# dt in the state-space units: multiplied per head into the product of decay and C·B

## The chip, the core and the metric

The kernel runs on one core of one Trainium2 chip. The time is the device time of one execution in microseconds; the median of several executions counts. Engines are named as in the profile: PE is TensorE, DVE is VectorE, ACT is ScalarE, POOL is GpSimd, SP is the engine that issues most of the DMAs; PEld is PE's loading of weights.

## What is computed

One layer of a decoder: a combined projection of 512 tokens, three token mixers side by side (DSA, NSA and a Mamba-2 state-space mixer, SSD), a gated sum and a feed-forward block. The change lies in the SSD mixer: 4 groups g of 8 heads, 4 chunks c of 128 tokens.

```python
def ssd_mixer(z, xbc, dt, conv_w, conv_b, dt_bias, a_log, d_skip, norm_g):
    ...
    seg = a_cum[:, :, :, None] - a_cum[:, :, None, :]
    lmat = jnp.exp(jnp.where(tril, seg, -jnp.inf))
    cb = jnp.einsum('bcign,bcjgn->bcijg', cm, bm)
    y_diag = jnp.einsum('bcijg,bcijgh,bcjgh,bcjghp->bcighp', cb, lmat, dtc, xs)
    decay_states = jnp.exp(a_cum[:, :, -1:] - a_cum)
    states = jnp.einsum('bcjgn,bcjgh,bcjghp->bcghpn', bm, decay_states * dtc, xs)
    ...
    y_off = jnp.einsum('bcign,bcghpn,bcigh->bcighp', cm, h_in, jnp.exp(a_cum))
    y = y_diag + y_off + xs * d_skip.reshape(SSD_GROUPS, SSD_HPG)[:, :, None]
    ...
    y = rms_norm(y * jax.nn.silu(z.astype(jnp.float32)), norm_g)
```

In y_diag, cb, the decay lmat, dt and x are multiplied and summed over the tokens j of the chunk. dt hangs on j and the head, as x does.

## The kernel before

The program is one stream of Python generators. `main()` runs the mixers one after the other: DSA, then SSD (`ssd`), then NSA. `filler()` makes the projections, the causal convolution, and later the branch and output projections. After each step of `main()` a loop lets `filler()` take steps until its share of work, a number that the step yields, is paid back. What is so recorded is then put in order for each engine by a scheduler with a timing of its own (`schedule_with_timeline_sim=True`), so a changed instruction can move others on every queue. PE runs its queue in the order given.

In the trace the SSD stage covers about 385 to 570 us. It has 16 units, one for a group and a chunk, numbered 0 to 15 here, in the order (0,0), (1,0), (0,1), (1,1) up to (1,3), then the same with groups 2 and 3. The fillers beside it are projections: groups of three products L451, L452 and L453 of 128x512 on PE, whose weights DVE splits at L172.

A unit works on chunk-by-chunk tiles with tokens on the partitions. `stage1` loads B, C (bcx) and the cumulated decays, spread to 128 partitions for 8 heads (E, three buffers). `load_xz` (L1257, issued by SP) loads x and z of the unit into one tile xz, of which there are two buffers: `u.xs` is its x half and `u.zs` its z half. `stage2` makes C·B in PSUM (`cbm`, tile name pv, L1264), masks E on POOL (L1265), takes eight exps on ACT (L1268, one per head) and multiplies E by `cbm` on DVE (L1275). POOL makes xt, x times dt (L1270, tile of its own, two buffers), xw for the state (L1273, not for the last chunk) and xd, x times the skip gain, which overwrites x (L1277).

`stage3` has the products of the state (L1286 reads it, L1293 makes the next one) and, for each of 8 heads, a 128x64 product of E and xt into the PSUM tile `py` (tile name sc, L1303). In the trace each head's product has two records. Then DVE adds the other terms (L1307) and multiplies by z (L1308), ACT squares the result for the norm and writes the square over z (L1309), and later PE transposes yv (L1314) for the store. The load of the unit after the next takes this unit's xz buffer, so it is issued after L1309.

The x of groups 2 and 3 are made by fillers while the units run: convolution on ACT and DVE (L821 to L828, its result is craw), transposes on PE (L835), a copy on ACT (L837) and a store that `load_xz` reads.

Of the kernel before, what the change touches and what calls it, by code (L numbers as in the profile page):

```python
# [7 lines left out]
F32 = mybir.dt.float32  # L8
F32R = mybir.dt.float32r
AF = mybir.ActivationFunctionType  # L10
ALU = mybir.AluOpType
# [29 lines left out]
def build_kernel(ctx, tc, A, out):  # L41
    nc = tc.nc
    pe, act, dve, pool = nc.tensor, nc.scalar, nc.vector, nc.gpsimd
# [5 lines left out]
    def bc(ap, shape):  # L49
        return ap.to_broadcast(shape)  # L50
# [6 lines left out]
    def popen(name, side="left", space=None, bufs=1):  # L57
        kw = dict(name=name, bufs=bufs, side=side)
        if space is not None:
            kw["space"] = space  # L60
            kw.pop("side")
        cm = tc.tile_pool(**kw)
        p = cm.__enter__()
        open_pools[name] = cm
        return p
# [24 lines left out]
    def ps(tag, shape, dt=F32, bufs=2):  # L90
        if tag == XT[0]:
            XT[1] += 1
            if XT[1] % 3 == 0:
                tag = "pF"
        return psp.tile(shape, dt, tag=tag, name=tag, bufs=PSB[tag])
# [17 lines left out]
    xt = []  # L113
# [1123 lines left out]
    def ssd(sv, ratio):  # L1237
        sp = popen("ssd", side="right")
        ssq = cp.tile([128, 4, 4], F32, name="ssq_y")
        col = lambda a, c, g: a[:, c * 32 + g * 8:c * 32 + g * 8 + 8]  # L1240
# [19 lines left out]
        def stage2(u):  # L1260
            g, c = u.g, u.c
            x3 = lambda a: a.rearrange("p (h d) -> p h d", d=64)
            cbm = ps("pv", [128, 512])[:, :128]
            pe.matmul(cbm, u.b[:, 0], u.b[:, 1], start=True, stop=True)  # L1264
            pool.affine_select(out=u.E, in_=u.E, compare_op=ALU.is_ge, fill=NEG, base=0,  # L1265
                               pattern=[[0, 8], [1, 128]], channel_multiplier=-1)
            for h in range(8):
                act.activation(u.E[:, h], u.E[:, h], AF.Exp, bias=col(sv["nac"], c, g)[:, h:h + 1])  # L1268
            u.xt = sp.tile([128, 512], F32, name="xt", bufs=2)
            pool.tensor_tensor(x3(u.xt), x3(u.xs), bc(col(sv["dth"], c, g)[:, :, None], [128, 8, 64]), op=ALU.mult)  # L1270
            if c < 3:
                u.xw = sp.tile([128, 512], F32, name="xw", bufs=2)
                pool.tensor_tensor(x3(u.xw), x3(u.xs), bc(col(sv["dw"], c, g)[:, :, None], [128, 8, 64]), op=ALU.mult)  # L1273
            yield ratio * 300
            dve.tensor_tensor(u.E, u.E, bc(cbm[:, None, :], [128, 8, 128]), op=ALU.mult)  # L1275
            u.xd = u.xs
            pool.tensor_tensor(x3(u.xd), x3(u.xs), bc(dskip[:, g * 8:g * 8 + 8][:, :, None], [128, 8, 64]), op=ALU.mult)  # L1277
            yield ratio * 300

        def stage3(u):  # L1280
            g, c = u.g, u.c
            x3 = lambda a: a.rearrange("p (h d) -> p h d", d=64)
            py = ps("sc", [128, 512])
            if c:
                po = ps("sc", [128, 512])
                pe.matmul(po, u.b[:, 1], hst[g], start=True, stop=True)  # L1286
                t1 = sp.tile([128, 512], F32, name="t1", bufs=2)
                dve.tensor_tensor(x3(t1), x3(po), bc(col(sv["ea"], c, g)[:, :, None], [128, 8, 64]), op=ALU.mult)
                pool.tensor_tensor(t1, t1, u.xd, op=ALU.add)
                yield ratio * 858  # L1290
            if c < 3:
                pst = ps("pT", [128, 512])
                pe.matmul(pst, u.b[:, 2], u.xw, start=True, stop=True)  # L1293
                hn = sp.tile([128, 512], F32, name="hst", bufs=4)
                if c == 0:
                    act.activation(hn, pst, AF.Copy)
                else:
                    pool.tensor_tensor(x3(hn), x3(hst[g]), bc(col(sv["dec"], c, g)[:, :, None], [128, 8, 64]), op=ALU.mult)
                    dve.tensor_tensor(hn, hn, pst, op=ALU.add)
                hst[g] = hn  # L1300
                yield ratio * 858
            for h in range(8):
                pe.matmul(py[:, h * 64:h * 64 + 64], u.E[:, h], u.xt[:, h * 64:h * 64 + 64], start=True, stop=True)  # L1303
                if h % 4 == 3:
                    yield ratio * 856
            yv = sp.tile([128, 512], F32, name="yv", bufs=2)
            dve.tensor_tensor(yv, py, t1 if c else u.xd, op=ALU.add)  # L1307
            dve.tensor_tensor(yv, yv, u.zs, op=ALU.mult)  # L1308
            act.activation(u.zs, yv, AF.Square, accum_out=ssq[:, c, g:g + 1])  # L1309

            def tr():
                pt = ps("pT", [128, 4, 128])
                for k in range(4):
                    pe.transpose(pt[:, k], yv[:, k * 128:k * 128 + 128], ident)  # L1314
                ev = sp.tile([128, 4, 128], F32, name="yev", bufs=2)
                for k in range(4):
                    act.activation(ev[:, k], pt[:, k], AF.Copy, scale=gcol[:, 4 * g + k:4 * g + k + 1])
                nc.sync.dma_start(yc_d[g, c], ev.rearrange("p k q -> p (k q)"))
            TR.append(tr)
            yield ratio * 100  # L1320
# [14 lines left out]
        yield from need(1)  # L1335
        load_xz(us[1])
        yield from stage2(us[0])
        for i in range(16):
            yield from need(i + 2)
            if i + 1 < 16:  # L1340
                yield from stage2(us[i + 1])
            if TR:
                TR.pop()()
                yield ratio * 436
            yield from stage3(us[i])
            if i + 2 < 16:
                load_xz(us[i + 2])
# [405 lines left out]
```

## Time and profile before

| | us |
|---|---|
| median of 3 runs | 1395.9 |
| lowest, highest | 1394.72, 1400.18 |
| profiled execution | 1403.27 |
| its span | 1401.5 |
| PE busy in the span | 1369.0 (98%) |
| DVE, ACT, POOL busy | 1001.1, 722.0, 286.8 |
| mean granted clock of PE, share of full | 0.986 |

The span is the profiled execution from its first to its last instruction. PE's clock has two levels, 1.2 and 2.4 GHz; the profile gives the granted clock of a stretch as a share of the higher one. An engine's busy time says little on its own here: what an edit is worth is read from the waits of PE in the stretch that it touches.

### The profile page before, as it was taken

To read this page: it belongs to the slowest core of one execution; us is meant where nothing else is said; L and a number is where in the kernel's file an instruction comes from. 1 tells how busy PE (TensorE), PEld (TensorE's weight loads), DVE (VectorE), ACT (ScalarE), POOL (GpSimd) and SP (SyncE) were. 2 spreads that over 40 slices of the span, in tenths; PEclk is the share of its full clock that TensorE was granted. 3 is DMA by queue.
4 is the path that set the end of the run, shared out by engine and by line. 5 is a ranking of instruction groups with operands and counts; after the bars stand their busy time and mean duration, and the time that the engine had idled before them with its cause. 6 is when DMAs were issued, how large, how long until landed. Compare 5 with 4: busy or idle time off the path is not lost.

```text
span 1401.5 us, 19674 instructions
## 1 busy us (share of the span) xinstructions
PE 1369.0 (98%) x6875; PEld 1142.1 (81%) x6875; DVE 1001.1 (71%) x1962; ACT 722.0 (52%) x1434; POOL 286.8 (20%) x235
## 2 busy tenths in 40 slices
PE   8989999999999999999999999999899999999998
PEld 7878888888877778888887888788789888888887
DVE  6499977999877656477667788888635575767841
ACT  5545436667666756366565566555224444444430
POOL 3445211111047375100000002133100201102000
PEclk9999999999999999999999999999999999999999
DMA  6335654644486687735435453435444665746531
GB/s 192 89 96 144 166 179 132 166 113 123 121 259 223 190 257 201 188 100 140 114 114 157 118 146 111 122 117 177 143 150 140 118 177 127 174 116 132 157 117 52
DMA packets 222721, 205.35 MB, mean 147 GB/s; under 512 B 15497, under 2 KB 170013, under 8 KB 222622
## 3 DMA queue, kind: packets, MB, share of 16 engines
q1 hardware_dynamic: 206652, 180.49, 43.7%
q0 software_dynamic: 15232, 20.98, 8.2%
q10 hardware_dynamic: 738, 2.63, 0.6%
q8 instruction: 54, 0.88, 0.3%
q14 instruction: 45, 0.37, 0.1%
HBM read 167.56 MB, written 36.51 MB: 146 GB/s over the span
## 4 chain that ended last, share of the span: by engine, by line
PE 77%; DVE 7%; DMA 7%; issue 4%; POOL 3%; ACT 2%; SPq 0%; DVEq 0%; POOLq 0%; ACTq 0%
PE pj L451 18%; PE pj L453 18%; PE pj L452 18%; PE sc L451 3%; PE sc L452 3%; PE sc L453 3%; DMA gld<-g_d 3%; PE pT L931 2%; PE sc L893 2%; PE sc L892 2%; PE pv L944 2%; DMA wraw<-in_w_in_dram 1%; PE pv L943 1%; POOL mixf L1488 1%; PE sc L1303 1%
## 5 line engine op out<-in xcount | busy, mean ns | idle before, releaser
L170 ACT ACTIVATE whi<-wraw 128x1024 fp32r<-128x1024 f32 (+2 forms) x190 | 198.3, 1048 | 233.8 <-PE pj L452 115.7
L172 DVE TENSOR_TENSOR wlo<-wraw,whi 128x1024 fp32r<-128x1024 f32 (+1 forms) x169 | 215.7, 1280 | 104.5 <-ACT whi L170 102.9
L451 PE MATMUL pj<-hTh,whi 128*128 128x512 f32 x384 | 153.6, 400 | 0.2 <-DVE cacc L824 0.2
L453 PE MATMUL pj<-hTh,wlo 128*128 128x512 f32 x384 | 152.6, 397 | 0.0
L452 PE MATMUL pj<-hTl,whi 128*128 128x512 f32 x384 | 152.3, 397 | 0.0
L451 PE MATMUL pj<-whi,hTh 128*128 128x512 f32 (+2 forms) x352 | 138.7, 394 | 5.9 <-DVE stk L521 3.2
L901 ACT ACTIVATE p<-p,nb,rs 128x256 f32<-128x256 f32 (+3 forms) x192 | 123.2, 645 | 30.6 <-DVE nb L899 30.6
L453 PE MATMUL pj<-whi,hTl 128*128 128x512 f32 (+2 forms) x352 | 137.8, 392 | 0.1
L452 PE MATMUL pj<-wlo,hTh 128*128 128x512 f32 (+2 forms) x352 | 137.6, 391 | 0.0
L451 PE MATMUL pj<-yh,whi 128*128 128x512 f32 (+1 forms) x288 | 109.7, 387 | 11.0 <-DVE gld L1485 6.4
L452 PE MATMUL pj<-yl,whi 128*128 128x512 f32 (+1 forms) x288 | 109.2, 379 | 0.0
L453 PE MATMUL pj<-yh,wlo 128*128 128x512 f32 (+1 forms) x288 | 108.9, 378 | 0.0
L452 PE MATMUL pj<-h2l,whi 128*128 128x512 f32 (+1 forms) x256 | 96.3, 376 | 0.0
L453 PE MATMUL pj<-h2h,wlo 128*128 128x512 f32 (+1 forms) x256 | 96.2, 376 | 0.0
L451 PE MATMUL pj<-h2h,whi 128*128 128x512 f32 (+1 forms) x256 | 96.1, 376 | 0.0
L987 POOL DMA_DIRECT2D qu<-q_d x32 | 23.5, 735 | 334.9 <-PE sc L893 259.3
L451 PEld LDWEIGHTS pj<-hTh,whi 128*128 128x128 f32 x384 | 72.4, 189 | 14.0 <-DVE cacc L824 0.4
L452 PEld LDWEIGHTS pj<-hTl,whi 128*128 128x128 f32 x384 | 72.4, 189 | 13.8 <-issue 0.5
L453 PEld LDWEIGHTS pj<-hTh,wlo 128*128 128x128 f32 x384 | 72.4, 189 | 13.8 <-issue 0.2
L451 PEld LDWEIGHTS pj<-whi,hTh 128*128 128x128 f32 x352 | 67.4, 192 | 19.8 <-issue 5.8
L935 ACT ACTIVATE pth<-pT 128x512 fp32r<-128x512 f32 x95 | 54.5, 592 | 47.4 <-PE pT L931 46.9
L453 PEld LDWEIGHTS pj<-whi,hTl 128*128 128x128 f32 x352 | 67.4, 191 | 12.4 <-DVE hTl L427 0.4
(385 smaller groups left out, 3294.9 us busy)
## 6 DMA issues: line engine op xcount, KB each, us to landing
wraw<-in_w_in_dram SPq DMA_DIRECT2D x84, 512.0 KB, 4.7
wraw<-in_w_ff_dram SPq DMA_DIRECT2D x58, 512.0 KB, 4.3
qd<-in_w_ff_dram POOLq DMA_DIRECT2D x18, 512.0 KB, 6.0
q_d<-qev SPq DMA_DIRECT2D x64, 128.0 KB, 2.5
qu<-q_d POOLq DMA_DIRECT2D x32, 256.0 KB, 3.7
E<-ac_d SPq DMA_DIRECT2D x16, 512.0 KB, 4.9
xz<-xz_d SPq DMA_DIRECT2D x16, 512.0 KB, 5.8
gld<-g_d SPq DMA_DIRECT2D x32, 256.0 KB, 2.8
```

Of the source, the lines that this page charges most:

```text
L170: act.activation(hi[:, :m], r[:, :m], AF.Copy)
L172: (pool if i in LOWP else dve).tensor_tensor(lo[:, :m], r[:, :m], f(hi[:, :m]), op=ALU.subtract)
L451: pe.matmul(o, lh, rh, start=first, stop=False)
L452: pe.matmul(o, lh, rl, start=False, stop=False)
L453: pe.matmul(o, ll, rh, start=False, stop=last)
L892: pe.matmul(s_[:, h % w, :n], u.q[h], kh[:, :n], start=True, stop=False)
L893: pe.matmul(s_[:, h % w, :n], u.q[h], kl[:, :n], start=False, stop=True)
L901: act.activation(u.p[h][:, :n], u.p[h][:, :n], AF.Exp, bias=u.nb[:, h:h + 1], scale=rs8[:, u.b, u.h0 + h:u.h0 + h + 1], accum_out=u.sm[:, ...
L931: pe.transpose(pt[:, h], u.p[h][:, kb * 128:kb * 128 + 128], ident)
L935: act.activation(ph, ptf, AF.Copy)
L944: pe.matmul(o, vk, pl0, start=False, stop=en)
L987: pool.dma_start(q.rearrange("p (i a) c -> p i (a c)", i=2), src)
```

## The change

POOL's product of x and dt (xt) is dropped. DVE's one product of E and C·B per unit, 128x1024, becomes eight instructions of 128x128, one for each head, that multiply E by the head's column of dt (dt's index j lies on the partitions of E) and by `cbm`. PE's products read x itself from xz. xd, which overwrote x, gets a tile of its own with two buffers, in the place that xt had. Lines after the removed one shift: L1273 is L1271, L1275 is L1274, L1277 is L1276, and L1286 to L1314 are one less.

```diff
--- before.py
+++ after.py
@@ -1266,14 +1266,13 @@
                                pattern=[[0, 8], [1, 128]], channel_multiplier=-1)
             for h in range(8):
                 act.activation(u.E[:, h], u.E[:, h], AF.Exp, bias=col(sv["nac"], c, g)[:, h:h + 1])
-            u.xt = sp.tile([128, 512], F32, name="xt", bufs=2)
-            pool.tensor_tensor(x3(u.xt), x3(u.xs), bc(col(sv["dth"], c, g)[:, :, None], [128, 8, 64]), op=ALU.mult)
             if c < 3:
                 u.xw = sp.tile([128, 512], F32, name="xw", bufs=2)
                 pool.tensor_tensor(x3(u.xw), x3(u.xs), bc(col(sv["dw"], c, g)[:, :, None], [128, 8, 64]), op=ALU.mult)
             yield ratio * 300
-            dve.tensor_tensor(u.E, u.E, bc(cbm[:, None, :], [128, 8, 128]), op=ALU.mult)
-            u.xd = u.xs
+            for h in range(8):
+                dve.scalar_tensor_tensor(u.E[:, h], u.E[:, h], col(sv["dth"], c, g)[:, h:h + 1], cbm, op0=ALU.mult, op1=ALU.mult)
+            u.xd = sp.tile([128, 512], F32, name="xd", bufs=2)
             pool.tensor_tensor(x3(u.xd), x3(u.xs), bc(dskip[:, g * 8:g * 8 + 8][:, :, None], [128, 8, 64]), op=ALU.mult)
             yield ratio * 300
 
@@ -1300,7 +1299,7 @@
                 hst[g] = hn
                 yield ratio * 858
             for h in range(8):
-                pe.matmul(py[:, h * 64:h * 64 + 64], u.E[:, h], u.xt[:, h * 64:h * 64 + 64], start=True, stop=True)
+                pe.matmul(py[:, h * 64:h * 64 + 64], u.E[:, h], u.xs[:, h * 64:h * 64 + 64], start=True, stop=True)
                 if h % 4 == 3:
                     yield ratio * 856
             yv = sp.tile([128, 512], F32, name="yv", bufs=2)
```

The scheduler orders every engine's queue anew from here on. PE at unit 0's output products; pj are the fillers' projections, sc the output products, pF the transposes of x for groups 2 and 3; the rows with - are before, those with + now:

```order
-L452 MATMUL pj<-hTl,whi 128x512
-L453 MATMUL pj<-hTh,wlo 128x512
-L451 MATMUL pj<-hTh,whi 128x512
-L1293 MATMUL pT<-xw,bcx 128x512
-L452 MATMUL pj<-hTl,whi 128x512
-L453 MATMUL pj<-hTh,wlo 128x512
-L1303 MATMUL sc<-xt,E 128x64 x2
+L1302 MATMUL sc<-xz,E 128x64 x2
+L1292 MATMUL pT<-xw,bcx 128x512
+L1302 MATMUL sc<-xz,E 128x64 x4
 L1264 MATMUL pv<-bcx 128x128
-L1303 MATMUL sc<-xt,E 128x64 x6
+L1302 MATMUL sc<-xz,E 128x64 x2
```

The unit's products stand five projection products earlier. The number of projection products between the last output product of unit i and the first of unit i+2, for i from 0 to 13, is 33, 31, 31, 33, 32, 30, 38, 92, 85, 29, 49, 56, 41, 36 before and 29, 36, 42, 36, 32, 33, 34, 92, 84, 19, 27, 34, 33, 33 now. From the last transposes of x (L835) to unit 9 it is 47 and 41. At the stage's last transposes the queue has 28 projection products fewer ahead; these stand later, beside NSA.

DVE at the end of unit 0, where L1307 and L1308 (now L1306 and L1307) finish the unit. Before:

```order
L1275 TENSOR_TENSOR E<-E,pv 128x1024
L172 TENSOR_TENSOR wlo<-wraw,whi 128x1024
L1307 TENSOR_TENSOR yv<-sc,xz 128x512
L1308 TENSOR_TENSOR yv<-yv,xz 128x512
L828 SCALAR_TENSOR_TENSOR craw<-cth,cacc 128x512
```

And now:

```order
L1274 SCALAR_TENSOR_TENSOR E<-E,sv_dth,pv 128x128 x7
L1306 TENSOR_TENSOR yv<-sc,xd 128x512
L1274 SCALAR_TENSOR_TENSOR E<-E,sv_dth,pv 128x128
L828 SCALAR_TENSOR_TENSOR craw<-cth,cacc 128x512
L1307 TENSOR_TENSOR yv<-yv,xz 128x512
L172 TENSOR_TENSOR wlo<-wraw,whi 128x1024
```

One of the next unit's eight pieces stands between the two steps that end unit 0, and the split of weights behind them.

POOL around units 3 and 4; hst is the state. Before:

```order
L1298 TENSOR_TENSOR hst<-hst,sv_dec 128x512
L1270 TENSOR_TENSOR xt<-xz,sv_dth 128x512
L1273 TENSOR_TENSOR xw<-xz,sv_dw 128x512
L1298 TENSOR_TENSOR hst<-hst,sv_dec 128x512
L1277 TENSOR_TENSOR xz<-xz,dskip 128x512
```

And now:

```order
L1297 TENSOR_TENSOR hst<-hst,sv_dec 128x512
L1265 AFFINE_SELECT E<-E 128x1024
L1288 TENSOR_TENSOR t_4217<-t_4217,xd 128x512
L1276 TENSOR_TENSOR xd<-xz,dskip 128x512
L1271 TENSOR_TENSOR xw<-xz,sv_dw 128x512
```

xd stands ahead of xw now, in the place of xt.

## Rows read from the trace of the kernel before

**Rows 1.** The page: busy time of each engine, and the chain that ended last.
```profile
PE 1369.0 (98%) x6875; PEld 1142.1 (81%) x6875; DVE 1001.1 (71%) x1962; ACT 722.0 (52%) x1434; POOL 286.8 (20%) x235
...
PE 77%; DVE 7%; DMA 7%; issue 4%; POOL 3%; ACT 2%; SPq 0%; DVEq 0%; POOLq 0%; ACTq 0%
```

**Rows 2.** Window 385:570: length, busy PE, PEld, DVE, ACT, POOL; PEclk, DMA share, GB/s.
```profile
385.00:570.00 185.00, 177.72 (x926) 142.64 (x925) 118.66 (x144) 116.83 (x301) 107.18 (x83) 0.97 0.75 227
```

**Rows 3.** PE's waits, 385 to 570: us in total, times, longest.
```profile
PE sc L1303 <- POOL xt L1270: 6.3, 4, 2.2
```

**Rows 4.** Windows of 5 and 10 us, columns as in rows 2.
```profile
420.00:425.00 5.00, 4.35 (x13) 2.56 (x14) 3.07 (x5) 1.33 (x5) 5.00 (x6) 0.66 0.82 255
465.00:470.00 5.00, 5.00 (x23) 4.53 (x24) 4.00 (x6) 4.05 (x14) 2.21 (x3) 0.67 0.95 347
495.00:505.00 10.00, 7.96 (x34) 5.93 (x35) 3.90 (x6) 2.49 (x4) 10.00 (x9) 0.83 0.54 168
```

**Rows 5.** Timeline, 411 to 421: start, length, engine, line; wait, releaser in brackets.
```profile
411.34 0.36 SPq L1257 DMA_DIRECT2D xz<-xz_d  x1
...
417.57 1.04 POOL L1270 TENSOR_TENSOR xt<-xz,sv_dth 128x512 f32<-128x512 f32 x1 [5.34 <-DMA xz<-xz_d]
...
418.67 0.88 PE L1303 MATMUL sc<-xt,E 128*128 128x64 f32 x6 [1.18 <-POOL xt L1270]
...
420.65 2.07 PE L1293 MATMUL pT<-xw,bcx 128*128 128x512 f32 x2 [0.66 <-POOL xw L1273]
```

**Rows 6.** Timeline, the three other waits for L1270.
```profile
437.70 1.04 POOL L1270 TENSOR_TENSOR xt<-xz,sv_dth 128x512 f32<-128x512 f32 x1 [4.57 <-DMA xz<-xz_d]
...
438.79 0.88 PE L1303 MATMUL sc<-xt,E 128*128 128x64 f32 x6 [1.16 <-POOL xt L1270]
...
462.56 1.15 POOL L1270 TENSOR_TENSOR xt<-xz,sv_dth 128x512 f32<-128x512 f32 x1 [3.81 <-DMA xz<-xz_d]
...
463.76 1.44 PE L1303 MATMUL sc<-xt,E 128*128 128x64 f32 x10 [1.77 <-POOL xt L1270]
...
494.78 2.08 POOL L1270 TENSOR_TENSOR xt<-xz,sv_dth 128x512 f32<-128x512 f32 x1 [10.46 <-DMA xz<-xz_d]
...
496.92 0.88 PE L1303 MATMUL sc<-xt,E 128*128 128x64 f32 x6 [2.18 <-POOL xt L1270]
```

**Rows 7.** Groups by line, 385 to 570: busy us, mean ns; idle before, releasers.
```profile
L1275 DVE TENSOR_TENSOR E<-E,pv 128x1024 f32<-128x1024 f32 x16 | 19.4, 1215 | 17.6 <-ACT E L1268 17.3 <-issue 0.2
...
L1270 POOL TENSOR_TENSOR xt<-xz,sv_dth 128x512 f32<-128x512 f32 x16 | 18.4, 1151 | 38.6 <-DMA xz<-xz_d 33.6 <-PE pj L453 5.0
```

**Rows 8.** Timeline of PE, two neighbouring projection products.
```profile
416.42 0.39 PE L453 MATMUL pj<-hTh,wlo 128*128 128x512 f32 x1
...
416.65 0.39 PE L451 MATMUL pj<-hTh,whi 128*128 128x512 f32 x1
```

**Rows 9.** Timeline, L1270 and L1303 of two units without a wait.
```profile
469.90 1.21 POOL L1270 TENSOR_TENSOR xt<-xz,sv_dth 128x512 f32<-128x512 f32 x1 [2.79 <-DMA xz<-xz_d]
...
473.60 0.78 PE L1303 MATMUL sc<-xt,E 128*128 128x64 f32 x6
...
510.68 1.04 POOL L1270 TENSOR_TENSOR xt<-xz,sv_dth 128x512 f32<-128x512 f32 x1 [1.92 <-DMA xz<-xz_d]
...
514.14 0.78 PE L1303 MATMUL sc<-xt,E 128*128 128x64 f32 x6
```

**Rows 10.** PE's waits, 570 to 1060, columns as in rows 3.
```profile
PE pj L451 <- ACT yh L807: 4.6, 2, 2.7
```

**Rows 11.** Timeline of DVE, 186 to 199: short instructions.
```profile
190.27 0.28 DVE L1197 SCALAR_TENSOR_TENSOR pre<-pre 128x128 f32<-128x128 f32 x1
190.47 1.21 DVE L172 TENSOR_TENSOR wlo<-wraw,whi 128x1024 fp32r<-128x1024 f32 x1
...
191.81 0.41 DVE L894 CUSTOM_DVE_ANT_0 p<-sc,mask 128x256 f32<-128x256 f32 x1
...
196.65 1.27 DVE L1197 SCALAR_TENSOR_TENSOR pre<-pre 128x128 f32<-128x128 f32 x4
```

## The prediction

> **What bounds the kernel now.** I read the page's busy times and its chain of work that ended last first. TensorE (PE) is busy for 98% of the span and carries 77% of that chain [rows 1], so an edit pays only where PE stands still or runs at its lower clock. The change removes no PE instruction: the same 128 products of 128x64 remain, with another right operand. VectorE (DVE) and GpSimd (POOL) are busy for 71% and 20% [rows 1]; time taken from POOL is worth nothing by itself.
>
> Next I read the stretch in which the state-space units run, 385 to 570 us. PE is busy for 177.72 of 185.00 us there, at a mean clock of 0.97, with DVE at 118.66 and POOL at 107.18 [rows 2]. All PE waits of note in the stretch are on this change's path: four waits of the output products at L1303 for the product of x and dt (L1270), 6.3 us [rows 3], and one of 0.7 us for L1273's product [rows 5]. So idle PE time is 185.00 − 177.72 = 7.3 us.
>
> Two of the five are about 2 us long or follow one another closely, and after three of these places the clock falls: the mean is 0.66 in 420 to 425, 0.67 in 465 to 470, and 0.83 in the ten from 495 to 505 [rows 4]. Before each, PE had stood still (418.67 and 420.65; 463.76; 496.92) [rows 5, 6]. Against full clock this is 5 x 0.34, 5 x 0.33 and 10 x 0.17, each about 1.7 us, 5.1 us in all. Idle and clock together, 7.3 + 5.1 = 12.4 us, are the ceiling of the gain in this stretch: 0.9% of the run.
>
> Then I read who releases each wait. A unit's tile xz (x and z) is one of two buffers, so the load for unit i+2 is issued only after the square of unit i (L1309), which follows its two DVE steps and its last product on PE. For unit 2 the load is issued at 411.34, x has landed when POOL starts at 417.57 (idle until then for the DMA), POOL takes 1.04 us, and PE goes on at 418.67 after waiting 1.18 [rows 5]. The other three look the same: landed 437.70, PE at 438.79; landed 462.56, PE at 463.76; landed 494.78, POOL 2.08 us long, PE at 496.92 [rows 6].
>
> **POOL's product removed.** Sixteen instructions of 1151 ns go, 18.4 us of POOL [rows 7]. The part on PE's path is the step between landing and PE: 1.1, 1.1, 1.2 and 2.1 us. Had PE come no earlier or later than before, it would have arrived at wait start, that is 418.67 − 1.18 = 417.49, 438.79 − 1.16 = 437.63, 461.99 and 494.74. Landings are at 417.57, 437.70, 462.56 and 494.78, so with x read directly the four waits would be 0.1, 0.1, 0.6 and 0.0 us: 0.8 for 6.3. That would be the gain if nothing else moved.
>
> **The order moves.** The scheduler puts fewer or more projection matmuls between a unit's last product and the first product of the unit two later, while the load's chain runs. Neighbouring ones start 0.23 us apart [rows 8], and a matmul fewer there brings PE to the wait that much earlier. Counted in the two programs' order, it falls for unit 2 from 33 to 29 (1.0 us earlier, wait 1.1); for unit 4 it rises from 31 to 42 (2.5 later, no wait); for unit 7 from 30 to 33 (0.7 later, no wait). Unit 8 has 34 for 38 (0.9 earlier), but x landed at 469.90 and PE came at 473.60 unwaiting [rows 9]: no wait. Unit 9's load hangs on x of its group being convolved, transposed and stored; from the last of those transposes there are 41 matmuls for 47, 1.4 us fewer, so its wait is 1.4. In the second half the counts fall most (29 to 19 at unit 11, 49 to 27 at unit 12), but margins are larger: unit 11's x landed at 510.68 and PE came at 514.14 [rows 9], 3.5 us against 2.3. The 0.7 us for L1273 stays: after the landing POOL now makes xd and then xw, where it made xt and then xw. For small waits I add 1.0 (0.2 that is there now, and the DVE term below). Removed waits: 7.3 − (1.1 + 1.4 + 0.7 + 1.0) = **3.1 us**, between 0 and 7.3. Of the three clock falls, the one at 465 goes with its wait, the one at 420 has 1.8 us of standing in two pieces as before, and the one at 500 has a shorter wait before it: between one and three remain, I take half, 1.5 x 1.7 = **2.5 us**.
>
> The matmuls taken out of this stretch (28 by its end, 6.4 us) run later beside the next mixer, whose queue ends where it did; PE's sum of work is the same. That neither gains nor costs, unless the waits there shift: PE waits 4.6 us in two places for the pieces of a mixer's output after 570 us [rows 10]. I allow ±3 us.
>
> **DVE's product in eight pieces.** One instruction of 1215 ns over 128x1024 [rows 7] becomes eight of 128x128 that also multiply by a column of dt. The nearest rows are L1197's: one lasts 0.28 us, and the next instruction starts 0.20 after it (190.27 to 190.47); four that depend on one another take 1.27 [rows 11]. Of independent heads I expect the first pitch: 7 x 0.20 + 0.28 = 1.7 us, 0.5 more per unit, some 8 us of DVE over 16 units. DVE is idle for 185.00 − 118.66 = 66 us of the stretch, which covers it. The bounds are 1.2 us, as before, 1.27 / 4 x 8 = 2.5 us for a dependent pitch, and, from a row with twice the elements that reads PSUM, 8 x 0.41 = 3.3 us [rows 11]. A piece can start once its own exp has ended, so behind the last exp only 0.3 us remain instead of 1.2; that product ends well before x lands in the four waits, so I cost this at nothing. The longer product matters through the queue: the DVE steps that end a unit (L1307, L1308) stand among such pieces, and half a microsecond there delays the next load by as much. At pitch 0.20 this adds at most some 0.4 us to each of unit 2's and unit 9's waits, which is in the 1.0 above.
>
> L1197's rows take all operands from SBUF, while one of the new instruction's lies in PSUM. The Trainium skill ("Perfetto Trace Analysis", section "Optimizing Scalar/DVE Operations") speaks against the change here: each DVE instruction carries an overhead of about 60 ns on SBUF and about 125 ns on PSUM, and grouping work into larger operations helps a saturated engine. By it seven more instructions would cost an estimated 7 x 125 ns = 0.9 us per unit and 14 us of DVE, still within the idle time, so it would move the sum by under a microsecond.
>
> **POOL's in-place write removed.** xd gets its own tile instead of overwriting x: the same 16 instructions. PE's products now read x itself, so the next load must also wait for them; they end before the square that it waits for anyway. Cost nothing; below nothing is excluded too, since POOL has no other waiter here than those counted.
>
> **Sum.** 1403.3 (profiled; its span is 1401.5) − 3.1 − 2.5 = 1397.7. The profiled execution lies 7.4 us above the median of 1395.9, so the forecast in the median's terms is 1395.9 − 5.6 = **1390.5 us** (rounded up by 0.2), with its own range 1386 to 1394.5.
>
> **Rivals.**
> All of it goes: the scheduler's shorter stretches never let PE arrive before x, all five waits and three falls end. For it: before, PE arrived within 0.6 us of the landing in all four. Against: four fewer matmuls at unit 2. It gives 1395.9 − 12 = 1384.
>
> One wait for another: the POOL step goes, PE comes as much earlier as the step was long and waits for the landing itself, and each standing still again ends in a fall of the clock. For it: the load alone takes 6.2 us from issue to landing (411.34 to 417.57 [rows 5]), whatever POOL does, and at units 2 and 9 PE does come earlier. Against: units 4 and 7, where it comes later. It gives about 1395.5.
>
> Slower, by DVE's pieces: at the pitch of the dependent rows a unit's pieces take 2.5 us, 1.3 more than before, and two units' pieces can stand ahead of L1307 or L1308, 2.6 us more for each link of the chain product, square, load, product. The waits become 1.1 + 2.6 = 3.7 at unit 2, about 2.5 at unit 7 (from a margin of 0.1), 1.4 + 2.6 = 4.0 at unit 9, 1.4 at unit 11 (margin 3.5 − 2.3), 0.2 at unit 4 (margin 2.4) and 0.7 for xw: 12.5 us, with four or five falls of 1.7 another 7.7. That is 20.2 − 12.4 = 7.8 more: 1404, the point from which this rival decides, at a pitch of about 0.32. At 0.41 two units' pieces add 4.2: 5.3, 4.1, 5.6, 3.0, 1.8 and 0.7 at the same places, 1.4 more at unit 8, 21.9 us, with seven falls 33.8, 21.4 more: 1417. Between the two I take 1410. The place is DVE's queue between 400 and 530 us. For it: the operand in PSUM, and the split of a unit's pieces around L1306 in the new order. Against: DVE's idle 66 us.
>
> **How the numbers follow.** Forecast 0.52, all gone 0.16, one for another 0.18, slower by pieces 0.14. A measurement of this kernel can tell 0.5%, 7 us, from no change: below 1388.9 is faster, above 1402.9 slower. Faster holds all of the second case and a little over a third of the first, 0.36; slower holds most of the last, 0.14; the rest, 0.50, is the same. The range leaves out nearly all of the slower rival and a little of the tails: 1383 to 1403; its lower end is the second case less 1 us.
>
> **What would show it.** Right: no POOL row between landing and PE, PE waits in the stretch at some 4 us and released by the DMA of xz itself, one or two falls of the clock, new DVE rows near 0.28 us with 0.20 us from one start to the next. Wrong: PE waits for DVE's pieces; waits for xz as long as before; a unit's chain from last product to landing of more than 14 us; or new waits after 570 us where the moved matmuls run. If idle plus clock loss in the stretch falls by 10 us, the second case holds; if the stretch gains but the end does not, the loss lies in the mixer behind it.

## The result and the profile after

The kernel with the change takes 1405.9 us (median of 6 runs, 1402.63 to 1406.79) beside 1395.98 of the kernel before in the same session: a ratio of 1.0062, 95% interval 1.0045 to 1.0078. A second session on another occasion gave 1.0041 (1.0025 to 1.0057; 1401.6 beside 1395.2). So it is slower by 0.4 to 0.6%, 6 to 10 us, where 1390.5 was forecast.

The two profiled executions hide this: 1402.63 us of after is its fastest run, and 1403.27 of before stood 7 us above its median. I therefore took a second trace of each, called b_again and a_again below.

The page of after, busy times and the chain that ended last:

```profile
PE 1364.5 (97%) x6875; PEld 1133.0 (81%) x6875; DVE 1014.4 (72%) x2074; ACT 720.1 (51%) x1434; POOL 273.9 (20%) x219
...
PE 72%; DMA 10%; DVE 6%; issue 4%; POOL 4%; ACT 3%; SPq 0%; DVEq 0%; POOLq 0%; ACTq 0%
```

Against [rows 1], PE's part of the chain fell from 77 to 72% and the DMA's rose from 7 to 10%. These shares tell little: in the second traces PE has 82% before and 72% after, the DMA 6 and 8%. POOL lost 13 us of work and DVE gained 13.

The stretch from 385 to 570 us, columns as in [rows 2], then PE's waits in it, as in [rows 3], all of after:

```profile
385.00:570.00 185.00, 177.33 (x940) 140.90 (x939) 134.75 (x261) 116.16 (x302) 96.11 (x71) 1.00 0.78 234
```

```profile
PE pT L1292 <- POOL xw L1271: 2.0, 2, 1.2
PE pT L1313 <- DVE yv L1307: 1.6, 2, 1.1
PE sc L1302 <- DMA xz<-xz_d: 1.3, 2, 0.9
PE sc L1028 <- DMA qu<-q_d: 1.3, 1, 1.3
PE pT L1313 <- ACT yev L1316: 1.0, 1, 1.0
```

The 6.3 us of waiting for POOL's product are gone, as forecast, and the wait for xz itself is small. But others stand in their place: for xw 2.0 us instead of 0.7, for DVE's last step of a unit 1.6 instead of 0.2 (but 2.8 in b_again). PE is idle for 7.7 us here, before 7.3. What was gained is the clock: 1.00 in this trace, 0.99 in a_again, where it was 0.97 in [rows 2] and in b_again. None of the single waits is as long as the 1.8 to 2.2 us behind which the clock fell in [rows 4 to 6]; that length alone does not decide it, the last section shows.

Unit 2 in after's timeline, which answers to [rows 5]:

```profile
416.84 1.30 PE L1302 MATMUL sc<-xz,E 128*128 128x64 f32 x10 [0.94 <-DMA xz<-xz_d]
416.87 1.61 POOL L1276 TENSOR_TENSOR xd<-xz,dskip 128x512 f32<-128x512 f32 x1 [3.29 <-DMA xz<-xz_d]
418.44 1.48 POOL L1271 TENSOR_TENSOR xw<-xz,sv_dw 128x512 f32<-128x512 f32 x1
```

PE's output products and POOL now start together when xz lands, and PE waits 0.94 us for it. DVE's eight pieces, as a group of the stretch (as in [rows 7]) and in the timeline:

```profile
L1274 DVE SCALAR_TENSOR_TENSOR E<-E,sv_dth,pv 128x128 f32<-128x128 f32 x128 | 35.2, 340 | 3.9 <-ACT E L1268 2.1 <-PE pv L1264 1.8
```

```profile
404.64 1.89 DVE L1274 SCALAR_TENSOR_TENSOR E<-E,sv_dth,pv 128x128 f32<-128x128 f32 x7
406.44 0.68 DVE L1306 TENSOR_TENSOR yv<-sc,xd 128x512 f32<-128x512 f32 x1
407.05 0.34 DVE L1274 SCALAR_TENSOR_TENSOR E<-E,sv_dth,pv 128x128 f32<-128x128 f32 x1
```

A piece lasts 0.34 us and seven take 1.89, so one starts (1.89 − 0.34) / 6 = 0.26 us after the other. Eight are some 2.2 us (35.2 / 16), for 1.2 of the one product before.

**Where the time went.** To compare traces with different orders I gave every PE record the median time from its start to the next one's for records of its kind, and summed these weights in the order of the trace: the sum is the work done. The time at which a trace reaches a given sum, less that sum, is what it has lost by then (only differences between kernels mean something). In us:

```
work done     before  b_again |  after  a_again
   400         10.4      9.1  |  11.1     11.0
   550         24.3     22.4  |  21.9     21.3
   825         32.4     26.8  |  24.9     25.4
  1000         24.3     16.9  |  23.8     24.7
  1375         13.7      6.2  |  13.2     14.1
```

From 400 to 550, the state-space stage, after loses 10.7 and 10.3 us where before loses 13.8 and 13.3: in these two traces of each the stage is 3 us faster. (A third pair, below, narrows this.) From 550 to 825 they lose 3 to 4.4 us, but for before's first trace with 8.1 (its wait of [rows 10] and a fall of the clock). From 825 to 1000, some 850 to 1020 us in the trace, before wins back 8.1 and 9.9 against the weights and after only 1.1 and 0.7. There it loses 7 to 9 us. In that stretch the last units of the next mixer (NSA) run beside the output projections, the branches: those of SSD in two halves, then NSA's own. None of the lines there is touched by the change. The experiments ask what happens in it.

### The profile page after: what moved, and what is told of

Its sections match the earlier page's. It is cut to its first block, busy times and chain, and to the rows that moved or that the text cites. A ratio compares the mean times of both kernels' runs of the same rounds, so it can differ in the third digit from the quotient of the medians.

```text
span 1400.6 us, 19777 instructions
## 1 busy us (share of the span) xinstructions
PE 1364.5 (97%) x6875; PEld 1133.0 (81%) x6875; DVE 1014.4 (72%) x2074; ACT 720.1 (51%) x1434; POOL 273.9 (20%) x219
## 4 chain that ended last, share of the span: by engine, by line
PE 72%; DMA 10%; DVE 6%; issue 4%; POOL 4%; ACT 3%; SPq 0%; DVEq 0%; POOLq 0%; ACTq 0%
PE pj L451 17%; PE pj L453 17%; PE pj L452 17%; PE sc L453 3%; PE sc L452 3%; PE sc L451 3%; PE pT L931 2%; DMA gld<-g_d 2%; PE sc L893 2%; PE sc L892 2%; PE pv L943 2%; PE pv L944 2%; POOL mixf L1487 2%; DMA xz<-xz_d 2%; DMA E<-ac_d 1%
## 5 line engine op out<-in xcount | busy, mean ns | idle before, releaser
L901 ACT ACTIVATE p<-p,nb,rs 128x256 f32<-128x256 f32 (+3 forms) x192 | 123.2, 644 | 35.2 <-DVE nb L899 35.1
L451 PE MATMUL pj<-yh,whi 128*128 128x512 f32 (+1 forms) x288 | 108.3, 382 | 13.3 <-DVE gld L1484 7.4
```

The costliest lines, as they stand in the source:

```text
L451: pe.matmul(o, lh, rh, start=first, stop=False)
L901: act.activation(u.p[h][:, :n], u.p[h][:, :n], AF.Exp, bias=u.nb[:, h:h + 1], scale=rs8[:, u.b, u.h0 + h:u.h0 + h + 1], accum_out=u.sm[:, ...
```

## The experiments

**First: which part of the change, and is the trace of before typical?** Four kernels on one chip. The first two are before and after again.

> The kernel before, unchanged, for a second trace and the clock of its runs. The profiled execution of before (1403.3 us, mean clock 0.986) stands 7 us above its median (1396). If it lost its time to the clock, the runs near 1396 show a clock of about 0.991 or more and fewer than three falls in 385 to 570 us (the ceiling of 12.4 us was then an outlier's). If the profile was typical, the runs near 1396 have a clock of 0.986 too. Time expected: 1396, ratio 1.000 +- 0.002.

> The kernel after, unchanged, for a trace of a typical run: 1402.6 and 1406 were both seen. If the loss lies behind the state-space stage (the 28 projection products that were moved there), the trace shows the stage at least 3 us ahead of before at equal work on PE and that lead gone by 1000 us. If it lies in DVE's pieces, the stage itself is behind. Time expected: 1403 to 1406.

b_again took 1395.3 us and its trace's clock is 0.991; a_again took 1401.6, less than the 1403 to 1406 expected, and its traced run, 1403.57, is the slowest of its eight. The stretch from 385 to 570 us of b_again, then of a_again, and PE's waits in b_again's:

```profile
385.00:570.00 185.00, 177.55 (x928) 142.55 (x927) 116.58 (x143) 117.30 (x302) 105.04 (x83) 0.97 0.76 227
385.00:570.00 185.00, 178.56 (x942) 142.58 (x942) 135.65 (x260) 116.71 (x302) 95.28 (x71) 0.99 0.76 233
```

```profile
PE sc L1303 <- POOL xt L1270: 4.1, 3, 2.2
PE pT L1314 <- DVE yv L1308: 2.8, 1, 2.8
```

In size b_again is as [rows 2]: 7.45 us idle and 0.97. So the loss that the prediction saw in the stage came again, and its outlier lost its time elsewhere (the clock, behind the wait of [rows 10] and later). But it is not made of the same waits: only 4.1 us are for POOL's product, and one of the two falls of the clock (there were three in the trace that was read) stands behind the 2.8 us for DVE's last step. a_again shows the lead of 3 us over the stage, and its loss behind it; that is in the table.

The third kernel does one part alone, the pieces:

```diff
-            dve.tensor_tensor(u.E, u.E, bc(cbm[:, None, :], [128, 8, 128]), op=ALU.mult)
+            for h in range(8):
+                dve.scalar_tensor_tensor(u.E[:, h], u.E[:, h], 1.0, cbm, op0=ALU.mult, op1=ALU.mult)
```

> Before, with DVE's product in eight pieces of 128x128 (times 1.0), POOL's product of x and dt kept. If the pieces are what costs, it is at 1403 to 1408. If they are hidden in DVE's idle time, it is at 1394 to 1398, and what the change lost comes from elsewhere. Its order on PE differs from both (the stage's last transposes stand behind 1653 projection products; 1666 before, 1638 after).

1397.3 us, a ratio of 1.0012 (1.0000 to 1.0023). The pieces cost 0.2% at most in this kernel, whose order on PE is neither before's nor after's; the rival that put a loss of 8 us and more on DVE's queue falls.

The fourth is after without the pieces. dt is brought in as a bias of the exp:

```diff
-        dve.tensor_scalar(sv["nac"], p[:, 0:128], -1.0, None, op0=ALU.mult)
+        act.activation(t["v"], sv["dth"], AF.Ln)
+        dve.tensor_tensor(sv["nac"], t["v"], p[:, 0:128], op=ALU.subtract)
...
-            for h in range(8):
-                dve.scalar_tensor_tensor(u.E[:, h], u.E[:, h], col(sv["dth"], c, g)[:, h:h + 1], cbm, op0=ALU.mult, op1=ALU.mult)
+            dve.tensor_tensor(u.E, u.E, bc(cbm[:, None, :], [128, 8, 128]), op=ALU.mult)
```

> After, but dt goes into the exp as a bias (the logarithm of dt, made once in the prelude), so that DVE's product is one instruction of 128x1024 again and POOL's product is still gone. By the pieces theory it comes to before's time or below (1388 to 1397). By the order theory (the stage's last transposes stand behind 1637 projection products, as in after with 1638, and the rest runs beside the next mixer) it is as slow as after: 1402 to 1406.

1399.1 us, 1.0032 (1.0019 to 1.0044): between the two, in neither of the ranges expected, and slower than before although in its units no engine has more to do than in before or after. Its trace has the best stage of the four kernels (7.3 us lost from 400 to 550) and the same loss behind it: −0.4 from 825 to 1000, where before has −8.1 and −9.9. This points to the order that dropping POOL's product brings about, and not to DVE's instructions.

**Second: is it the order alone?** One number, R3, says how much filler work a state-space unit asks for. It changes no instruction, only where the queues have them. Before with R3 = 1.0 happens to get after's order behind the stage (from 700 us on the two traces' order differs in some 20 records of PE and 2 of DVE):

```diff
-R0, R1, R2, R3 = 1000.0, 1.5, 2.5, 0.5
+R0, R1, R2, R3 = 1000.0, 1.5, 2.5, 1.0
```

> Before, with one number changed: R3, the share of filler work that a state-space unit asks for, 1.0 for 0.5. No computation is changed; POOL's product stays and DVE's is one instruction. In the order on PE the stage then ends after 1635 projection products (before 1666, after 1638), and the next mixer's eight units start after 1702, 1778, 1845, 1974, 2148, 2256, 2436, 2561 of them, against 1733, 1815, 1887, 2021, 2176, 2278, 2438, 2573 before and 1704, 1791, 1863, 1985, 2148, 2256, 2436, 2561 after. If the loss of after is the shift of the mixer behind against its fillers, this is slower than before too: 1399 to 1404. If the loss belongs to what the change does in the units, it stays at 1393 to 1397.

After with R3 = 0.7 and 0.9 gets nearly that of before, counted by the projection products ahead of each of the next mixer's units (the same line with 0.7 and 0.9), and with 0.55 it keeps its own:

> After, with R3 0.7 for 0.5. The next mixer's units then start after 1734, 1820, 1895, 2024, 2178, 2298, 2438, 2598 projection products, nearly as before. If the shift is the cause, the loss behind the stage is gone and the gain of the stage is kept: 1390 to 1396. If the change's own instructions are the cause, 1400 to 1404 stays.

> After, with R3 0.9: the next mixer's units start after 1733, 1815, 1886, 2033, 2180, 2287, 2438, 2598 projection products, again nearly as before, but with another order inside the state-space stage. By the theory of the shift 1390 to 1397, by that of the change's own instructions 1400 to 1404.

> After, with R3 0.55: a control. The order inside the state-space stage differs, the next mixer's units start after 1698, 1776, 1857, 1994, 2148, 2256, 2436, 2561 projection products, as early as in after. By the theory of the shift it stays slow, 1399 to 1404; if any change of order scatters the time by some us without regard to that shift, it may land anywhere from 1390 to 1406.

All four times came out as the order says. Before with another R3: 1403.5 us, 1.0060 (1.0040 to 1.0080), as slow as after with nothing of the change in it. After with R3 0.7: 0.9999 (0.9984 to 1.0015); with 0.9: 0.9986 (0.9972 to 1.0000); with 0.55: 1.0038 (1.0022 to 1.0055). From 825 to 1000 the traces lose, in the measure of the table, +0.7 (before, R3 1.0) and −2.2 (after, 0.55), against −13.2 and −12.1 (after, 0.7 and 0.9). The gain of the stage, which the expectation for 0.7 wanted kept, is not there. Its stretch from 385 to 570 us has 8.0 us of idle PE and a clock of 0.96:

```profile
385.00:570.00 185.00, 177.03 (x917) 142.46 (x916) 130.36 (x252) 115.52 (x300) 92.68 (x68) 0.96 0.72 224
```

Then I looked for what stands still in that stretch. DVE's waits from 850 to 905 us (engine, tile and line, what it waited for: us in total, times, longest), of b_again:

```profile
DVE p L894 <- PE sc L893: 3.3, 3, 1.3
DVE gld L1462 <- DMA gld<-g_d: 3.2, 2, 2.2
```

of after:

```profile
DVE gld L1461 <- DMA gld<-g_d: 8.5, 3, 3.8
DVE yl L808 <- ACT yh L807: 2.6, 2, 2.2
```

and of before with R3 1.0:

```profile
DVE gld L1462 <- DMA gld<-g_d: 9.0, 3, 3.7
DVE yl L808 <- ACT yh L807: 1.6, 2, 1.2
```

In before DVE waits there for PE's scores (L893), which is as it should be where PE is the bound. In the two slow kernels DVE stands for 8.5 to 9 us, in three waits, at one line, the multiplication of a freshly loaded gate (gld) by the norm, and what is queued behind it stands too: the softmax of NSA and the split of the next branch's input (yl). PE's own waits in the same stretch of after are for that input above all, and little for the softmax's maximum (mx):

```profile
PE pj L451 <- ACT yh L807: 4.3, 3, 2.3
PE sc L892 <- DVE mx L894: 0.6, 2, 0.5
```

After's timeline shows the ring:

```profile
847.97 2.21 POOL L1487 TENSOR_TENSOR mixf<-mixf,gld 128x512 f32<-128x512 f32 x1 [5.50 <-DVE gld L1486]
849.06 0.37 SPq L152 DMA_DIRECT2D wraw<-in_w_br_ssd_dram  x1
850.21 0.34 SPq L1385 DMA_DIRECT2D gld<-g_d  x1
854.95 0.69 DVE L1461 SCALAR_TENSOR_TENSOR gld<-gld,rtok 128x512 f32<-128x512 f32 x1 [3.11 <-DMA gld<-g_d]
...
856.17 0.45 PE L892 MATMUL sc<-kh_w,qu 128*128 128x384 f32 x1 [0.48 <-DVE mx L894]
```

POOL frees one of the two gate buffers at 850.18, SP issues the gate's load at once, at 850.21, and it lands some 4.7 us after that. DVE had reached L1461 at 851.8, only 1.6 us behind the issue, and has waited 3.11 us. Then PE waits 0.48 us for the maximum that stood behind it. The same place in b_again:

```profile
844.92 1.29 POOL L1488 TENSOR_TENSOR mixf<-mixf,gld 128x512 f32<-128x512 f32 x1 [5.03 <-DVE gld L1487]
846.24 0.34 SPq L1386 DMA_DIRECT2D gld<-g_d  x1
849.19 0.38 SPq L152 DMA_DIRECT2D wraw<-in_w_br_ssd_dram  x1
849.69 0.68 DVE L1462 SCALAR_TENSOR_TENSOR gld<-gld,rtok 128x512 f32<-128x512 f32 x1
```

Here too the gate's load goes directly behind POOL (846.21), but DVE comes to its multiplication 3.45 us behind the issue, and the load has landed. In after SP had issued a load of weights ahead of the gate's, here it issues it behind; whether that makes the landing later is not shown.

**Third: is that wait the cause?** The multiplication by the norm need not stand before PE's product. Written the other way round, the first instruction that reads the gate needs PE's product too, and DVE is not sent to wait for the load ahead of its time:

```diff
-                if br[0] == "c":
-                    dve.scalar_tensor_tensor(th, th, 1.0, R, op0=ALU.add, op1=ALU.mult)
...
-                if br[0] == "b":
-                    dve.scalar_tensor_tensor(th, th, 1.0, p, op0=ALU.add, op1=ALU.mult)
-                else:
-                    dve.tensor_tensor(th, th, p, op=ALU.mult)
+                dve.scalar_tensor_tensor(th, th, 1.0, p, op0=ALU.add, op1=ALU.mult)
+                if br[0] == "c":
+                    dve.tensor_tensor(th, th, R, op=ALU.mult)
```

This was put into after, before, the kernel with the bias, and after with R3 0.9.

> After, with one step of the branch outputs behind the state-space stage written otherwise. The gate of a branch is loaded into gld; in the SSD branch DVE first multiplies the loaded gate by the norm (L1461, it waits for the load) and later by PE's product. Here the product comes first and the norm second, so that nothing on DVE waits for the load before PE's product is there. PE's order is that of after up to the SSD branch. If DVE, standing at that instruction for the load (8.5 us in after, 3.2 in before, between 855 and 905 us), is what holds PE up in after, 3 to 5 us come back: 1397 to 1400. If those waits of DVE are only bystanders, 1401 to 1404 stays.

> Before, with the same rewriting of the gate. DVE stood there for 3.2 us only, so at most 1 to 2 us should come back: 1393 to 1396; about the same as before.

> dt as a bias of the exp (one product on DVE, none on POOL), with the rewriting of the gate: the same order behind the stage as in after. If the gate is the main part of the loss, 1399 goes to 1394 to 1396; if not, 1398 to 1400.

> After with R3 0.9 (the fastest so far, 1393.3) and the rewriting of the gate. DVE's waits for the gate were 2.6 us there, so at most 1 us: 1392 to 1394.

The ratios are to before on the same chip in the same session.

| kernel | without | ratio to before | with the gate rewritten | ratio to before |
|---|---|---|---|---|
| before | 1395.3 | 1 | 1393.4 | 0.9978 (0.9967 to 0.9989) |
| after | 1401.6 | 1.0041 (1.0025 to 1.0057) | 1394.4 | 0.9984 (0.9971 to 0.9996) |
| dt as a bias | 1399.1 | 1.0032 (1.0019 to 1.0044) | 1389.6 | 0.9959 (0.9945 to 0.9973) |
| after, R3 0.9 | 1393.3 | 0.9986 (0.9972 to 1.0000) | 1389.2 | 0.9956 (0.9941 to 0.9971) |

After wins back 7 us, more than the 3 to 5 expected; the kernel with the bias 9.5 us, where at most 5 were expected. Before gains 2.5 us (1393.4 beside 1395.8 in its session), where 1 to 2 were expected, and after with R3 0.9 gains 4 us, where 1 was expected. DVE's waits from 850 to 905 us in after with the gate rewritten are before's again, and the one at the gate is short and for PE:

```profile
DVE p L894 <- PE sc L893: 3.6, 3, 2.4
...
DVE gld L1481 <- PE pj L453: 0.9, 1, 0.9
```

From 825 to 1000 this kernel loses −10.3 where after lost −1.1 and −0.7. Up to 809 us the order of PE is after's, record for record, so what had shifted by then costs nothing by itself. But the scheduler also orders anew what follows the rewriting: some 600 of PE's 6875 records stand elsewhere behind 809 us, in the very stretch of the loss. This run does not tell the end of DVE's wait from that new order. For the wait speaks that the kernels in which DVE had stood for 8 to 9 us (after, and the one with the bias) won 7 and 9.5 us, and those in which it had stood for 3.2 and 2.6 us (before, and after with R3 0.9) won 2.5 and 4. Against it speaks that these two won more than was expected as well, so a part of what the rewriting gives comes from something else.

What the expectation missed is the branch's second half and NSA's branch behind it. PE's waits from 570 to 1060 us, of after:

```profile
PE pj L451 <- DVE gld L1484: 7.4, 7, 2.3
PE pj L451 <- ACT yh L807: 5.8, 6, 2.3
PE pj L452 <- DVE yl L808: 1.1, 1, 1.1
```

and of after with the gate rewritten:

```profile
PE pj L451 <- DVE gld L1481: 7.9, 7, 1.7
PE pj L451 <- ACT yh L807: 2.3, 3, 1.5
```

The waits for a branch's input (yh, yl) fall from 6.9 to 2.3 us; these inputs are loaded into a ring of two buffers that DVE's split frees. That they came late behind the gates is read from the kernel and not followed wait by wait. Those for gld at the end of the branches (7.4 and 7.9) stay, in both. PE's listed waits from 570 to 1060 us are 15.1 us in after, 11.3 in b_again and 11.4 here, so they explain some 4 of the 7 to 9 us; where the rest lies I have not followed.

The two kernels with the gate rewritten keep the order of before and of after on PE and DVE up to some 800 us, so their traces are a third pair for the stage. The stretch from 385 to 570 us of before with the gate rewritten, then of after with it:

```profile
385.00:570.00 185.00, 177.42 (x937) 142.45 (x936) 119.33 (x142) 116.93 (x302) 110.27 (x85) 0.99 0.76 230
385.00:570.00 185.00, 177.10 (x935) 141.11 (x935) 134.90 (x257) 116.98 (x303) 96.16 (x71) 0.99 0.76 229
```

Here the stage of after gains nothing. Idle time and clock loss together (the clock in windows of 2.5 us against full) are 12.4, 12.6 and 9.3 us in the three traces of before's stage and 7.7, 8.2 and 9.6 in those of after's: some 3 us less on the mean, with ranges that overlap, and all of it clock. At the end, too, after with the gate rewritten stands at 1394.4 beside before's 1393.4, with intervals that overlap. So even with the loss behind the stage gone, the change itself shows no gain.

The last two kernels of the table are faster than before and after. Whether R3 0.9 with the bias and the gate together would be faster still was not run.

## Why the prediction was wrong, step by step

**What bounds the kernel** held: PE, and in the stage its waits and the clock behind them. But the ceiling of 12.4 us was read from one trace. b_again has 12.6, of which 2.8 us are a wait for DVE's last step, off the change's path; the third trace of the same order has 9.3.

**POOL's product removed** held in its place: no POOL instruction lies between landing and the output products any more, and unit 2 waits 0.94 us for xz (1.08 in a_again) where 1.1 was worked out (1.0 by its own rows: four products of 0.23 us are 0.9). Unit 9's wait of 1.4 us for xz did not come; 1.15 us for its xw stands there. In a_again unit 11 waits 1.40 us for xz, where none was forecast. The waits for xz in the stage are 1.3 us together in after and 2.8 in a_again. Unit 9 of after, then unit 11 of a_again:

```profile
495.83 1.12 PE L1292 MATMUL pT<-xw,bcx 128*128 128x512 f32 x2 [1.15 <-POOL xw L1271]
508.52 1.75 PE L1302 MATMUL sc<-xz,E 128*128 128x64 f32 x14 [1.40 <-DMA xz<-xz_d]
```

**Removed waits, 3.1 us**, was too much: the idle time of the stage is 7.7, 6.4 and 7.9 us in the three traces of after's order, where it was 7.3, 7.45 and 7.6. So next to nothing went. I added 1.0 us for waits not foreseen, and in the first trace there were some 5: for xw (2.0 instead of 0.7), for the end of a unit on DVE (1.6), for the copy of the transposes (1.0) and at the next mixer's start (1.3).

**The clock, 2.5 us**, is near the mean of what came, and that is luck: the loss was 5.1, 5.1 and 1.7 us in the three traces of before's stage and none, 1.7 and 1.7 in those of after's, so one pair shows 5 us and another none. With both steps the stage gained some 3 us on the mean, where 5.6 was forecast.

**The matmuls moved out of the stage** is the step that failed. "That neither gains nor costs, unless the waits there shift", with ±3 us: they shifted, by 7 to 9 us, and turned the sign. Before with R3 1.0, which has that order and nothing of the change, is 0.6% slower too. DVE's wait at the gate is a part of it; how large a part, beside the rest of the new order, is not told apart. I had looked at PE's own waits of [rows 10] and at the end of PE's queue, which was the same, and not at the queue of DVE beside the branches, where an instruction that waits for a load moved ahead of NSA's work. The order of DVE there was to be had before the run. So was a hint in the trace: DVE waited for the gate there in before too, from 850 to 905 us by 3.4:

```profile
DVE gld L1462 <- DMA gld<-g_d: 3.4, 2, 2.1
```

**DVE's pieces**: the pitch was taken as 0.20 us from L1197 [rows 11] and is 0.26; 2.2 us a unit for 1.7. The step was mis-sized but hidden, as it said: pieces alone give 1.0012. The Trainium skill ("Perfetto Trace Analysis", section "Optimizing Scalar/DVE Operations") has about 125 ns of overhead for a DVE instruction that reads PSUM; the estimate from it, 1.2 + 7 x 0.125 = 2.1 us, is some 0.1 us below the run. The row that I preferred gave too little; its operands all lie in SBUF, but no run here shows that this is why. With the gate rewritten the kernel with the bias and one product stands at 0.9959 and after at 0.9984. That may be the pieces, but some 590 of PE's records stand elsewhere in the stage of the two, so it is not shown.

**The rivals.** None of them was what happened. The one on the slower side had the right engine, DVE, at the wrong place: its queue between 400 and 530 us, not between 850 and 960. That the time came out where it put it, between 1404 and 1410, is chance: the stage in which it saw the loss lost nothing. One wait for another is half true of the stage. The forecast of "what would show it" did name the case, a stage that gains and a loss in the mixer behind.

**The range** was too narrow by the same step: ±3 us for a reordering of the rest of the program. One number that only reorders moved this kernel from 1395 to 1403.5.

## What to carry to other kernels

Where a scheduler orders the queues, an edit has two prices: its own, read from the stage that it touches, and that of the new order of all that follows, which here was two to three times as large and of the other sign. The first takes more than one trace: the gain of this stage lay in its clock, and that differed between executions of the same order. A control that reorders without computing anything else (one share, one priority) costs one run and tells the two apart. Look in every in-order queue for instructions that wait for a load and stand ahead of work that PE needs, and write them so that their first operand to come late is the one that PE makes.

## What was not expected of the hardware

PE's clock stayed at 1.00 over the whole stage of after with 7.7 us of waits in it, the longest 1.3 us, while in before falls of the clock followed the places with 1.8 to 2.2 us of standing [rows 4 to 6]. The length of a wait does not decide it alone, though. In a_again the clock fell behind 1.08 us, at the place where after had waited 0.94 and kept it; and in after it held behind 2.27 us. First a_again, PE's wait and the stretch behind it, then after:

```profile
416.86 1.30 PE L1302 MATMUL sc<-xz,E 128*128 128x64 f32 x10 [1.08 <-DMA xz<-xz_d]
420.00:422.50 2.50, 2.50 (x7) 1.53 (x6) 2.50 (x4) 0.00 (x0) 2.50 (x2) 0.53 0.74 226
```

```profile
898.73 0.73 PE L451 MATMUL pj<-yh,whi 128*128 128x512 f32 x2 [2.27 <-ACT yh L807]
900.00:905.00 5.00, 4.18 (x21) 2.99 (x20) 4.68 (x21) 3.59 (x10) 0.00 (x0) 1.00 0.41 109
```

So one order of instructions can lose the clock in one execution and keep it in the next; what decides is not shown here.
